# High and low parts of weights and activations side by side, two elements apart, at eight rotating offsets

## The chip, the cores and the metric

The kernel runs on one core of a Trainium2 chip. The metric is the device time of one execution in microseconds (us). Each execution computes one layer of an encoder trunk, from inputs in HBM to an output in HBM.

## The reference

All arithmetic is float32. Sequence length S is 256, model width D is 2048, MLP width 8192, and the memory has 256 tokens. The layer is a chain of matrix products with short work between them:

```python
h = rms_norm(x, norm_mix_g)
x = x + hybrid_mixer(h, ...)                       # one product with w_in (2048 x 18464), then w_out
h = rms_norm(x, norm_x_g); mem_n = rms_norm(mem, norm_mem_g)
x = x + cross_attention(h, mem_n, w_xq, w_xkv, w_xo)   # 4 heads
h = rms_norm(x, norm_ffn_g)
x = x + square(relu(h @ w_ff1)) @ w_ff2
return rms_norm(x, norm_final_g)
```

`hybrid_mixer` splits the product with w_in into a retention branch and a gated delta-rule branch, both worked in chunks along the sequence, gates them and adds them. Every weight is read once: 404 MB cross the DMA queue in one execution.

## The kernel before

A float32 product is made of three faster ones. Each operand is split into a high part, which is the value rounded to the format `float32r`, and a low part, which is the rest; high*high, high*low and low*high are summed in PSUM. ScalarE (ACT) makes the high part by a copy, VectorE (DVE) the low part by a subtraction.

**Weights.** `fetch` (L87) loads 1 MB of a weight matrix with one DMA into the tile `raw` (128 x 2048, three buffers) and splits it in two halves of 128 x 1024: L106 writes the high half `whi` on ACT, L107 the low half `wlo` on DVE. Both are tiles of their own with three buffers each. `whi` has room for 64 elements more, and in `blocks` it starts 56 elements (224 bytes) into its buffer (`AT_BLOCKS`); in `chunk` it starts at 0. All tile sizes of that pool are multiples of 256 bytes, so this fixes where each operand lies within a period of 256 bytes.

**Activations.** A `Quad` (L124) holds four k-tiles of the activations, feature-major. Its tile `both` is 128 x 4 x 512: for each k-tile first 256 high elements (one per token), then 256 low ones. Quads live in the pools `hq` (`quad_a`), `q2` (`quad_b`) and, for the memory's activations, `kv` (`memq`, L293). Two empty tiles, `PAD1` (8 elements) and `PAD2` (80), shift the last two pools.

**Two forms of a product.** TensorE (PE) loads a stationary operand of 128 x 128 (LDWEIGHTS, shown as PEld) and streams a moving operand of up to 512 columns past it; the load for the next matmul goes on while the present one streams.

- `blocks` (L171): the weights are stationary, the output is feature-major. Per k-tile and output block, L187 streams the whole 512 columns (high and low activations at once) past the high weights, and L188 streams the 256 high activations past the low weights. It makes the mixer's q, k, v and decay inputs, the memory's keys, w_out, w_xq, w_xo and the MLP's first product.
- `chunk` (L133): the activations are stationary, the output is token-major. Per k-tile and half of the tokens, L147, L148 and L149 stream 512 weight columns each: high*high, high*low, low*high. It makes the memory's values (4 calls, on `memq`), the mixer's values and gates (20 calls, on `h1`), and the MLP's second product (16 calls, on `hid`).

Each of these matmuls has its own LDWEIGHTS. The order of the instructions on each engine is set by the tile framework, which schedules with a simulated timeline and the priorities that the code gives; PE then works strictly in that order.

Of the kernel before, what the change touches and what calls it, by code (L numbers as in the profile page):

```python
# [11 lines left out]
F32R = mybir.dt.float32r  # L12
# [5 lines left out]
P = 128  # L18
D = 2048
S = 256  # L20
# [10 lines left out]
THETA = 10000.0  # L31


AT_BLOCKS = (56, 0)
PAD1, PAD2 = 8, 80
TWO_PI = 2.0 * math.pi
BIG = 1.0e30
# [14 lines left out]
def trunk(ctx: ExitStack, tc: tile.TileContext, x, mem, positions, norm_mix_g, w_in, conv_w, gdn_a_log, gdn_dt_bias,  # L52
# [8 lines left out]
    wp = ctx.enter_context(tc.tile_pool(name="wpipe", bufs=3))  # L61
    hqp = ctx.enter_context(tc.tile_pool(name="hq", bufs=1))
# [4 lines left out]
    def stream_ps():  # L67
        s0 = psp.tile([P, 512], F32, name="s0", tag="s0", bufs=2)
        s1 = psp.tile([P, 512], F32, name="s1", tag="s1", bufs=2)
        return s0, s1  # L70

    def bank():
        return psp.tile([P, 512], F32, name="b", tag="b", bufs=4)
# [4 lines left out]
    def step():  # L78
        if steps and next(steps[0], steps) is steps:
            steps.pop(0)  # L80
# [3 lines left out]
            step()  # L84


    def fetch(pieces, k, n, rush=False, hold=None, at=(0, 0)):  # L87


        raw = wp.tile([P, k * n], F32, name="raw", tag="raw", bufs=3)  # L90
        rv = raw.rearrange("p (k n) -> p k n", k=k)
        with tc.high_priority(offset=100000):
            for off, ap in pieces:
                src = ap.rearrange("(k p) n -> p k n", p=P)
                for ks in ((slice(0, k // 2), slice(k // 2, k)) if rush else (slice(0, k),)):
                    nc.sync.dma_start(rv[:, ks, off:off + ap.shape[1]], src[:, ks, :])
            got = []
            for i in range(2):
                if hold:
                    both = hold().both  # L100
                    hi, lo = (both[:, a:a + 2, :].rearrange("p a s -> p (a s)") for a in (0, 2))
                else:
                    hi, lo = (wp.tile([P, k * n // 2 + room], F32R, name=nm, tag=nm, bufs=3)[:, a:a + k * n // 2]
                              for nm, a, room in zip(("whi", "wlo"), at, (64, 0)))
                src = raw[:, i * k * n // 2:(i + 1) * k * n // 2]
                act.activation(hi, src, AF.Copy)  # L106
                vec.tensor_sub(lo, src, hi.bitcast(F32))  # L107
                got.append((hi.rearrange("p (k n) -> p k n", n=n), lo.rearrange("p (k n) -> p k n", n=n)))
        return got

    def split(dst, src, at=slice(None)):
        h, l = (a[:, at] for a in dst)
        act.activation(h, src, AF.Copy)
        vec.tensor_sub(l, src, h.bitcast(F32))
# [6 lines left out]
    class Quad(tuple):  # L121
        pass

    def new_quad(pl, bufs):  # L124
        both = pl.tile([P, 4, 2 * S], F32R, name="q", tag="q", bufs=bufs)
        quad = Quad((both[:, :, 0:S], both[:, :, S:2 * S]))
        quad.both = both
        return quad

    def quad_a():  # L130
        return new_quad(hqp, 5)

    def chunk(quads, pieces_of, evac, before=None, hold=None):  # L133


        ps = stream_ps()
        parts = [(t, 0, 512, ps[t]) for t in range(NT)]
        if hold:
            parts[1:] = [(1, 0, 256, ps[1][:, :256]), (1, 256, 512, bank()[:, :256])]
        held = {q: fetch(pieces_of(q), 4, 512, hold=hold) for q in ((2, 3) if hold else ())}  # L140

        def products(q, i, part, halves):
            t, c0, c1, o = part
            xh, xl = (a[:, i, t * P:(t + 1) * P] for a in quads[q])
            wh, wl = (a[:, i % 2, c0:c1] for a in halves[i // 2])
            first, last = q == 0 and i == 0, q == 3 and i == 3
            pe.matmul(o, xh, wh, start=first, stop=False)  # L147
            pe.matmul(o, xh, wl, start=False, stop=False)  # L148
            pe.matmul(o, xl, wh, start=False, stop=last)  # L149

        for q in range(4):
            if q not in held:
                if before:
                    before(q)
                halves = fetch(pieces_of(q), 4, 512, rush=before is not None and q == 0)
                for i in range(4):
                    for part in parts:
                        products(q, i, part, halves)
                    if i % 2:
                        step()  # L160
        for part in parts:
            for q, halves in held.items():
                for i in range(4):
                    products(q, i, part, halves)
            with tc.high_priority(offset=50000):
                evac(part[0], part[3], part[1], part[2])
# [4 lines left out]
    def blocks(quads, w, c0, nb, evac):  # L171

        k = 16 // nb
        ps = stream_ps()
        n = nb * P
        for g in range(KT // k):
            halves = fetch([(0, w[g * k * P:(g + 1) * k * P, c0:c0 + n])], k, n, at=AT_BLOCKS)
            for i in range(k):  # L180
                kk = g * k + i
                xh, xhl = quads[kk // 4][0][:, kk % 4, :], quads[kk // 4].both[:, kk % 4, :]
                wh, wl = halves[i // (k // 2)]
                for b in range(nb):
                    bs = slice(b * P, (b + 1) * P)
                    lh, ll = wh[:, i % (k // 2), bs], wl[:, i % (k // 2), bs]
                    pe.matmul(ps[b], lh, xhl, start=kk == 0, stop=False)  # L187
                    pe.matmul(ps[b][:, :S], ll, xh, start=False, stop=kk == KT - 1)  # L188
                if i % (k // 2) == k // 2 - 1:
                    step()  # L190
        for b in range(nb):
            with tc.high_priority(offset=50000):
                o = sm.tile([P, S], F32, name="bo", tag="bo", bufs=2)
                act.activation(o, ps[b][:, S:], AF.Copy)  # L194
                vec.tensor_add(o, o, ps[b][:, :S])  # L195
                evac(b, o)
# [73 lines left out]
    kv = kvs.enter_context(tc.tile_pool(name="kv", bufs=2))  # L270
# [19 lines left out]
    kt_d = dram.tile([P, KT, S], F32, name="kt_d", tag="kt_d", bufs=1)  # L290
    vv_d = dram.tile([P, NT, D], F32, name="vv_d", tag="vv_d", bufs=1)
    kv.tile([P, PAD1], F32, name="pad1", bufs=1)
    memq = [new_quad(kv, 4) for _ in range(4)]  # L293
    ssqm = cp.tile([P, NT, 4], F32, name="ssqm")

    def load_mem(c):
# [31 lines left out]
    for k2 in range(8):  # L328
# [10 lines left out]
        for f in range(2):  # L339
            k = 2 * k2 + f  # L340
# [160 lines left out]

    values(2)
    blocks(h1, w_in[0], C_GA, 1, decay_rows)
    values(3)
    for h in range(4):
# [6 lines left out]
    for b2 in range(8):  # L512
        ko = kv.tile([P, 2, S], F32, name="ko", tag="vo", bufs=2)

        def evac_k(b, ps):
            vec.tensor_mul(ko[:, b, :], ps, mrow)

        blocks(memq, w_xkv[0], b2 * 256, 2, evac_k)
        nc.sync.dma_start(kt_d[:, 2 * b2:2 * b2 + 2, :], ko)
        if b2 < 4:  # L520
            for h in (2 * b2, 2 * b2 + 1):
                decays(8 + h)
                ret_decays(h)
# [17 lines left out]
    def gdn_stream(grp):  # L541
# [3 lines left out]
        for pr in range(2):  # L545
# [5 lines left out]
            for part, c0, bofs in ((1, C_GQ, 0), (0, C_GK, 16), (2, C_GV, 32)):  # L551
                def evac(b, ps, part=part, bofs=bofs):
                    if part < 2:
                        conv_silu(bofs + h0 + b, ps, kq[:, b, part, :])
                    else:
                        vt = mx.tile([P, S], F32, name="vt", tag="vt", bufs=2)
                        conv_silu(bofs + h0 + b, ps, vt)
                        vts.append(vt)
                blocks(h1, w_in[0], c0 + h0 * GD, 2, evac)
# [260 lines left out]
    for j in range(5):  # L820
# [3 lines left out]
        if j:  # L824
            if j < 4:
                quad = mx.tile([P, 4, S], F32, name="mg", tag="mg", bufs=3)
                kept.append(quad)
            else:
                finish_steps()
                quad = quad_a()  # L830
# [21 lines left out]
    def quad_b():  # L852
        return new_quad(q2p, 4)
# [49 lines left out]
    for h in range(XH):  # L903
# [31 lines left out]
        quad = quad_a()  # L935
        for d2 in range(2):
            ops = bank()
            ov = ops.rearrange("p (d s) -> p d s", d=2)
            for d in range(2):
                c0 = (2 * d2 + d) * P  # L940
# [24 lines left out]
    for fb in range(4):  # L965
        hid = []
        for b2 in range(8):
            hs = fp.tile([P, 2, S], F32, name="hs", tag="hs", bufs=2)
            if b2 % 2 == 0:
                hid.append(quad_a())  # L970

            def evac_h(b, ps):
                vec.scalar_tensor_tensor(hs[:, b, :], ps, 0.0, ps, op0=ALU.max, op1=ALU.mult)  # L973
                qh, ql = (a[:, b2 % 2 * 2 + b, :] for a in hid[-1])
                act.activation(qh, hs[:, b, :], AF.Copy)  # L975
                vec.tensor_sub(ql, hs[:, b, :], qh.bitcast(F32))  # L976

            blocks(h3, w_ff1[0], fb * D + b2 * 256, 2, evac_h)
        for n in range(4):
# [13 lines left out]
            def evac_last(t, ps, c0, c1):  # L993
# [20 lines left out]
                for c in (0, 3, 1, 2):  # L1014
# [13 lines left out]
                  hold=quad_b if last else None)  # L1028
# [27 lines left out]
```

## Time and profile before

| | |
|---|---|
| runs | 2108.81 us median of 2 (2108.48 to 2109.13) |
| profiled execution | 2106.88 us, span of its instructions 2105.2 us |
| PE busy | 2083.3 us (99%), 11172 matmuls |
| DVE busy | 1407.7 us (67%) |
| ACT busy | 1091.6 us (52%) |
| DMA | 193 GB/s in the mean, queue q1 59.5% of 16 engines |
| granted TensorE clock | 0.999 |

In a row of the groups stand the line, engine and operation, then output and inputs by tile name, their shapes, the count, the busy time with the mean of one in ns, and the idle time of the engine before them with what ended it. A matmul's duration in the profile holds its latency through the array, so the rate of a stream of matmuls is read from the distance between their starts in the timeline, not from the duration.

### The profile page before, as it was taken

Reading aid. Unit: us, or ns where it says so; the run is one execution under the profiler, and the core shown is the slowest. Engines: PE = TensorE matmul, PEld = TensorE weight load, DVE = VectorE, ACT = ScalarE, POOL = GpSimd, SP = SyncE. Lnnn points to the kernel's source line nnn. Section 1 sums busy time; section 2 is a strip of 40 time slices with the busy share of each in tenths; the row PEclk is TensorE's granted clock in tenths of the full one; section 3 lists DMA queues with packets and bytes.
Section 4 is the critical chain, followed back from the end, with each engine's and each line's share of the span. In section 5 each row is a group of like instructions: output and inputs, shape, how many; then the busy total and the mean of one; then the engine's idle time right before and its main releaser. Section 6 shows DMA issues by size and latency. Waiting matters only on the chain.

```text
span 2105.2 us, 28781 instructions
## 1 busy us (share of the span) xinstructions
PE 2083.3 (99%) x11172; PEld 1796.9 (85%) x11172; DVE 1407.7 (67%) x2225; ACT 1091.6 (52%) x1700; POOL 28.7 (1%) x39
## 2 busy tenths in 40 slices
PE   8999999999999999999999999999999999999998
PEld 6878888888888888888888899888888888888887
DVE  6756779678758884878557666766556555645655
ACT  7565564565446454655355555554434434434444
POOL 0000000000000000000000000000000000000000
PEclk9999999999999999999999999999999999999999
DMA  8778655555545555555458654566566556556653
GB/s 298 243 242 258 201 181 193 176 171 182 184 156 193 192 175 166 182 183 190 153 174 256 202 186 155 180 197 186 199 190 191 197 187 197 188 192 198 185 198 140
DMA packets 316010, 405.91 MB, mean 193 GB/s; under 512 B 16593, under 2 KB 224481, under 8 KB 315745
## 3 DMA queue, kind: packets, MB, share of 16 engines
q1 hardware_dynamic: 315872, 404.08, 59.5%
q8 instruction: 87, 1.43, 0.3%
q14 instruction: 51, 0.41, 0.1%
HBM read 390.40 MB, written 13.65 MB: 192 GB/s over the span
## 4 chain that ended last, share of the span: by engine, by line
PE 93%; DMA 3%; ACT 2%; DVE 1%; SPq 1%; issue 0%; ACTq 0%; POOLq 0%; POOL 0%; DVEq 0%
PE s L187 32%; PE s L188 17%; PE s L148 13%; PE s L149 13%; PE s L147 13%; PE b L675 2%; DMA dec_d<-dec_w 1%; ACT whi L106 1%; DVE wlo L107 1%; ACT dec_w L493 1%; PE b L581 1%; DMA xc<-x 1%; PE b L117 0%; DMA xt_d<-xt 0%; PE b L119 0%; PE b L118 0%
## 5 line engine op out<-in xcount | busy, mean ns | idle before, releaser
L107 DVE TENSOR_TENSOR wlo<-raw,whi 128x1024 fp32r<-128x1024 f32 x702 | 858.3, 1223 | 522.0 <-ACT whi L106 516.2
L106 ACT ACTIVATE whi<-raw 128x1024 fp32r<-128x1024 f32 x702 | 742.3, 1059 | 730.9 <-PE s L149 387.0
L187 PE MATMUL s<-q,whi 128*128 128x512 f32 x3088 | 1063.4, 390 | 0.7 <-ACT whi L106 0.4
L188 PE MATMUL s<-q,wlo 128*128 128x256 f32 x3088 | 845.3, 281 | 5.2 <-DVE wlo L107 5.1
L187 PEld LDWEIGHTS s<-q,whi 128*128 128x128 f32 x3088 | 570.8, 188 | 111.5 <-ACT whi L106 1.6
L188 PEld LDWEIGHTS s<-q,wlo 128*128 128x128 f32 x3088 | 579.0, 188 | 20.1 <-DVE wlo L107 8.8
L148 PE MATMUL s<-wlo,q 128*128 128x512 f32 x1264 | 495.6, 392 | 1.0 <-DVE wlo L107 1.0
L149 PE MATMUL s<-whi,q 128*128 128x512 f32 x1264 | 492.4, 390 | 0.0
L147 PE MATMUL s<-whi,q 128*128 128x512 f32 x1264 | 454.1, 391 | 0.0
L148 PEld LDWEIGHTS s<-wlo,q 128*128 128x128 f32 x1264 | 238.0, 188 | 50.1 <-DVE wlo L107 2.5
L147 PEld LDWEIGHTS s<-whi,q 128*128 128x128 f32 x1264 | 237.5, 188 | 49.2 <-ACT q L249 0.4
L149 PEld LDWEIGHTS s<-whi,q 128*128 128x128 f32 x1264 | 237.6, 188 | 48.0
L194 ACT ACTIVATE bo<-s 128x256 f32<-128x256 f32 x193 | 73.1, 379 | 118.8 <-PE s L188 105.9
L195 DVE TENSOR_TENSOR bo<-bo,s 128x256 f32<-128x256 f32 x193 | 80.4, 417 | 44.4 <-ACT bo L194 44.1
L534 DVE SCALAR_TENSOR_TENSOR acc<-bo,cw,acc 128x255 f32<-128x255 f32 (+2 forms) x144 | 66.8, 480 | 1.5
L636 DVE TENSOR_TENSOR pr<-lw,tw 32x31 f32<-32x31 f32 (+15 forms) x124 | 40.4, 325 | 8.4 <-DMA lw<-scr_l 6.5
L638 DVE TENSOR_TENSOR tw<-tw,pr 32x31 f32<-32x31 f32 (+15 forms) x124 | 40.5, 327 | 2.1
L782 ACT ACTIVATE gth<-s 128x512 f32<-128x512 f32 x32 | 18.9, 591 | 22.5 <-PE s L149 18.3
L984 DVE SCALAR_TENSOR_TENSOR res<-s,rstd3q,res 128x512 f32<-128x512 f32 (+1 forms) x32 | 22.3, 735 | 11.8 <-PE s L149 11.8
L973 DVE SCALAR_TENSOR_TENSOR hs<-bo 128x256 f32<-128x256 f32 x64 | 27.0, 422 | 1.1
L976 DVE TENSOR_TENSOR q<-hs,q 128x256 fp32r<-128x256 f32 x64 | 26.8, 419 | 0.8 <-ACT q L975 0.8
L531 ACT ACTIVATE acc<-bo,cw 128x256 f32<-128x256 f32 x48 | 24.1, 503 | 4.5 <-DVE bo L195 4.4
(292 smaller groups left out, 1084.3 us busy)
## 6 DMA issues: line engine op xcount, KB each, us to landing
raw<-w_in SPq DMA_DIRECT2D x144, 1024.0 KB, 5.1
raw<-w_ff SPq DMA_DIRECT2D x128, 1024.0 KB, 5.4
raw<-w_xkv SPq DMA_DIRECT2D x31, 1024.0 KB, 5.9
raw<-w_out SPq DMA_DIRECT2D x16, 1024.0 KB, 5.7
raw<-w_xq SPq DMA_DIRECT2D x16, 1024.0 KB, 6.5
raw<-w_xo SPq DMA_DIRECT2D x16, 1024.0 KB, 5.5
dec_d<-dec_w SPq DMA_DIRECT2D x16, 192.0 KB, 4.0
dec<-dec_d SPq DMA_DIRECT2D x8, 384.0 KB, 3.2
```

Source lines behind the costliest of these rows:

```text
L106: act.activation(hi, src, AF.Copy)
L107: vec.tensor_sub(lo, src, hi.bitcast(F32))
L147: pe.matmul(o, xh, wh, start=first, stop=False)
L148: pe.matmul(o, xh, wl, start=False, stop=False)
L149: pe.matmul(o, xl, wh, start=False, stop=last)
L187: pe.matmul(ps[b], lh, xhl, start=kk == 0, stop=False)
L188: pe.matmul(ps[b][:, :S], ll, xh, start=False, stop=kk == KT - 1)
L194: act.activation(o, ps[b][:, S:], AF.Copy)
L195: vec.tensor_add(o, o, ps[b][:, :S])
L534: vec.scalar_tensor_tensor(acc[:, d:], ps[:, :S - d], cw[:, j, blk:blk + 1], acc[:, d:], op0=ALU.mult, op1=ALU.add)
L638: vec.tensor_sub(tw[:, j + 1:32, 0:j + 1], tw[:, j + 1:32, 0:j + 1], pv)
L675: pe.matmul(pv[:, i, :], lhs(i), rhs[:, i, :], start=True, stop=True)
```

## The change

The high and the low part of a tile now lie in one tile, element by element (high, low, high, low, ...), for the weights of `blocks`, for the MLP's hidden activations and for the memory's activations. Every operand that reads one part then has a step of two elements (8 bytes). The weights of `chunk`, and the activations `h1`, `h2`, `h3`, the attention's and the merged ones keep one part behind the other.

- As **stationary** operands with that step: the weights in all calls of `blocks` (L187, L188, now L202, L203), and the activations in 20 of 40 calls of `chunk` (L147 to L149, now L161 to L163): 16 of the MLP, 4 of the memory.
- As **moving** operands with that step: `memq` in the 8 calls of `blocks` that make the memory's keys.
- The tiles `whi` and `wlo` become one tile `w` (128 x 2112, three buffers). Its parts start at an offset that goes through eight values, 0 to 56 elements in steps of 8, from one call of `blocks` or `chunk` to the next; `AT_BLOCKS` goes. The two pads stay as they are.

```diff
-AT_BLOCKS = (56, 0)
+AT_WEIGHTS = (0, 8, 16, 24, 32, 40, 48, 56)
...
+                    w = wp.tile([P, 2 * half + 64], F32R, name="w", tag="w", bufs=3)[:, at:at + 2 * half]
+                    w = w.rearrange("p (n e) -> p e n" if mixed else "p (e n) -> p e n", e=2)
+                    hi, lo = w[:, 0], w[:, 1]
                 act.activation(hi, src, AF.Copy)
                 vec.tensor_sub(lo, src, hi.bitcast(F32))
...
+    def next_at():
+        used.append(0)
+        return AT_WEIGHTS[len(used) % len(AT_WEIGHTS)]
...
+    def sides(both, mixed):
+        return both.rearrange("p f (s e) -> p f e s" if mixed else "p f (e s) -> p f e s", e=2)
...
-            halves = fetch([(0, w[g * k * P:(g + 1) * k * P, c0:c0 + n])], k, n, at=AT_BLOCKS)
+            halves = fetch([(0, w[g * k * P:(g + 1) * k * P, c0:c0 + n])], k, n, at=at, mixed=True)
...
-                xh, xhl = quads[kk // 4][0][:, kk % 4, :], quads[kk // 4].both[:, kk % 4, :]
+                xh, xhl = quads[kk // 4][0][:, kk % 4, :], quads[kk // 4].pair[:, kk % 4]
...
-    memq = [new_quad(kv, 4) for _ in range(4)]
+    memq = [new_quad(kv, 4, mixed=True) for _ in range(4)]
...
-                hid.append(quad_a())
+                hid.append(quad_a(mixed=True))
```

The number and the sizes of the matmuls, splits and DMAs stay the same. The schedule moves a little. On PE, in a call of `blocks` for the memory's keys (`s0`, `s1` are the two output blocks, `q` the activations), the order before was:

```order
827 L187 MATMUL s0_1901<-q_98,whi_1905 128x512
828 L188 MATMUL s0_1901<-q_98,wlo_1906 128x256
829 L187 MATMUL s1_1902<-q_98,whi_1905 128x512
830 L188 MATMUL s1_1902<-q_98,wlo_1906 128x256
831 L187 MATMUL s0_1901<-q_98,whi_1905 128x512
```

and it is now:

```order
827 L202 MATMUL s0_1843<-q_98,w_1847 128x512
828 L202 MATMUL s1_1844<-q_98,w_1847 128x512
829 L203 MATMUL s0_1843<-q_98,w_1847 128x256
830 L203 MATMUL s1_1844<-q_98,w_1847 128x256
831 L202 MATMUL s0_1843<-q_98,w_1847 128x512
```

At the first k-tile of a new half of weights the two products with the high part now stand ahead of the two with the low part; after that the pairs alternate as before. Two products with the high part followed each other at 141 places of `blocks` before, at 298 now.

More of the change, by code (lines that the diff above doesn't have):

```diff
@@ L84, in finish_steps, with fetch @@
             step()
-    def fetch(pieces, k, n, rush=False, hold=None, at=(0, 0)):
+    def fetch(pieces, k, n, rush=False, hold=None, at=0, mixed=False):
         raw = wp.tile([P, k * n], F32, name="raw", tag="raw", bufs=3)
@@ L97, in fetch @@
             got = []
+            half = k * n // 2
             for i in range(2):
+                src = raw[:, i * half:(i + 1) * half]
                 if hold:
@@ L102, in fetch @@
                 else:
-                    hi, lo = (wp.tile([P, k * n // 2 + room], F32R, name=nm, tag=nm, bufs=3)[:, a:a + k * n // 2]
-                              for nm, a, room in zip(("whi", "wlo"), at, (64, 0)))
-                src = raw[:, i * k * n // 2:(i + 1) * k * n // 2]
+                    w = wp.tile([P, 2 * half + 64], F32R, name="w", tag="w", bufs=3)[:, at:at + 2 * half]
+                    w = w.rearrange("p (n e) -> p e n" if mixed else "p (e n) -> p e n", e=2)
+                    hi, lo = w[:, 0], w[:, 1]
                 act.activation(hi, src, AF.Copy)
@@ L109, in fetch @@
         return got
+    used = []
+    def next_at():
+        used.append(0)
+        return AT_WEIGHTS[len(used) % len(AT_WEIGHTS)]
     def split(dst, src, at=slice(None)):
@@ L122, in trunk, with new_quad, quad_a @@
         pass
-    def new_quad(pl, bufs):
+    def sides(both, mixed):
+        return both.rearrange("p f (s e) -> p f e s" if mixed else "p f (e s) -> p f e s", e=2)
+    def new_quad(pl, bufs, mixed=False):
         both = pl.tile([P, 4, 2 * S], F32R, name="q", tag="q", bufs=bufs)
-        quad = Quad((both[:, :, 0:S], both[:, :, S:2 * S]))
-        quad.both = both
-        return quad
-    def quad_a():
-        return new_quad(hqp, 5)
+        pair = sides(both, mixed)
+        quad = Quad((pair[:, :, 0], pair[:, :, 1]))
+        quad.both, quad.pair = both, pair
+        return quad
+    def quad_a(mixed=False):
+        return new_quad(hqp, 5, mixed)
     def chunk(quads, pieces_of, evac, before=None, hold=None):
@@ L139, in chunk @@
             parts[1:] = [(1, 0, 256, ps[1][:, :256]), (1, 256, 512, bank()[:, :256])]
+        at = next_at()
         held = {q: fetch(pieces_of(q), 4, 512, hold=hold) for q in ((2, 3) if hold else ())}
@@ L154, in chunk @@
                     before(q)
-                halves = fetch(pieces_of(q), 4, 512, rush=before is not None and q == 0)
+                halves = fetch(pieces_of(q), 4, 512, rush=before is not None and q == 0, at=at)
                 for i in range(4):
@@ L177, in blocks @@
         n = nb * P
+        at = next_at()
         for g in range(KT // k):
-            halves = fetch([(0, w[g * k * P:(g + 1) * k * P, c0:c0 + n])], k, n, at=AT_BLOCKS)
+            halves = fetch([(0, w[g * k * P:(g + 1) * k * P, c0:c0 + n])], k, n, at=at, mixed=True)
             for i in range(k):
                 kk = g * k + i
-                xh, xhl = quads[kk // 4][0][:, kk % 4, :], quads[kk // 4].both[:, kk % 4, :]
+                xh, xhl = quads[kk // 4][0][:, kk % 4, :], quads[kk // 4].pair[:, kk % 4]
                 wh, wl = halves[i // (k // 2)]
```

## The prediction

> **What bounds the kernel now.** I read the page first, for shares and groups, then the list of waits of PE, then PE's timeline for the rate of its matmuls, and last the busy times by window for the engines that feed it.
>
> ```profile
> span 2105.2 us, 28781 instructions
> PE 2083.3 (99%) x11172; PEld 1796.9 (85%) x11172; DVE 1407.7 (67%) x2225; ACT 1091.6 (52%) x1700; POOL 28.7 (1%) x39
> L107 DVE TENSOR_TENSOR wlo<-raw,whi 128x1024 fp32r<-128x1024 f32 x702 | 858.3, 1223 | 522.0 <-ACT whi L106 516.2
> L106 ACT ACTIVATE whi<-raw 128x1024 fp32r<-128x1024 f32 x702 | 742.3, 1059 | 730.9 <-PE s L149 387.0
> L187 PE MATMUL s<-q,whi 128*128 128x512 f32 x3088 | 1063.4, 390 | 0.7 <-ACT whi L106 0.4
> L188 PE MATMUL s<-q,wlo 128*128 128x256 f32 x3088 | 845.3, 281 | 5.2 <-DVE wlo L107 5.1
> L148 PE MATMUL s<-wlo,q 128*128 128x512 f32 x1264 | 495.6, 392 | 1.0 <-DVE wlo L107 1.0
> ```
>
> PE has work in 99% of the span. The idle time just before its large groups is 0.7, 5.2 and 1.0 us. The splits wait for PE instead: ACT stood idle 387.0 us until an L149 had released a buffer. So what PE needs per matmul sets the time, and everything else matters only if it makes PE wait. The rate of a matmul is the distance between starts. In the MLP's first product (`blocks`):
>
> ```profile
> 1428.08 0.39 PE L187 MATMUL s<-q,whi 128*128 128x512 f32 x1
> 1428.31 0.28 PE L188 MATMUL s<-q,wlo 128*128 128x256 f32 x1
> 1428.42 0.39 PE L187 MATMUL s<-q,whi 128*128 128x512 f32 x1
> ...
> 1433.24 0.39 PE L187 MATMUL s<-q,whi 128*128 128x512 f32 x1
> ```
>
> and at the end of a `chunk`, where a call of `blocks` follows, at two places:
>
> ```profile
> 505.29 0.39 PE L149 MATMUL s<-whi,q 128*128 128x512 f32 x1
> 505.52 0.39 PE L147 MATMUL s<-whi,q 128*128 128x512 f32 x1
> 505.75 0.39 PE L148 MATMUL s<-wlo,q 128*128 128x512 f32 x1
> 505.97 0.40 PE L149 MATMUL s<-whi,q 128*128 128x512 f32 x1
> 506.21 0.39 PE L187 MATMUL s<-q,whi 128*128 128x512 f32 x1
> ...
> 1744.31 0.39 PE L147 MATMUL s<-whi,q 128*128 128x512 f32 x1
> ...
> 1745.44 0.40 PE L149 MATMUL s<-whi,q 128*128 128x512 f32 x1
> 1745.68 0.39 PE L187 MATMUL s<-q,whi 128*128 128x512 f32 x1
> ```
>
> From 1428.08 to 1433.24 stand 15 pairs of L187 and L188: 5.16 / 15 = 0.344 us a pair. In `chunk`, 505.29 to 505.97 is three matmuls, 0.227 us each, and 1744.31 to 1745.44 is five, 0.226 each. If a 512-column stream takes 0.227 in `blocks` as well, the 256-column one takes 0.117. The second 256 columns then cost 0.110, so of each matmul about 0.117 - 0.110 = 0.007 us does not grow with its length.
>
> The last matmul of each chunk is the one to look at. Its own weights lie at offset 0 of their buffer; while it streams, PE loads the first weights of `blocks`, which lie 224 bytes further in the period. It takes 0.24 us at both places, against 0.227 and 0.226 just before. The timeline's last digit is 0.01 us, so I count this as 0.008 more: about the mean of the two, cut a little for the rounding. In the streams of 0.227 both operands lie at the same place of the period. So the trace shows that a load which lies elsewhere than the stream can slow the stream by a few per cent. It shows no operand of PE with a step of two.
>
> **The change, part by part.** The instructions, their sizes and the DMAs stay. What changes is how PE reads, how ACT and DVE write, and where things lie.
>
> *Stationary operands with the step: blocks.* All 3088 L187 and 3088 L188 now stream past weights that were loaded with a step of 8 bytes over 1024 bytes instead of 512, at eight offsets in turn. Bound below: the load and the stream no longer touch, and the 0.007 us that does not grow with the length goes: 3088 x 2 x 0.007 = 43 us gained. Bound above: the load passes twice as many bytes, and each stream pays the 0.008 twice: 3088 x 2 x 0.016 = 99 us lost. The nearest row is the 0.24: a load out of place. With a step the load moves through the period differently from the stream, so I take its price, 0.008, for every 512-column stream: 3088 x 0.008 = 24.7 us. The 256-column stream already runs beside a load that lies 224 bytes away and takes 0.117, no more than the slope gives; for it I take 0.002, near its lower bound: 6.2 us.
>
> *Stationary operands with the step: chunk.* 20 of 40 calls, each 16 k-tiles x 2 halves x 3 = 96 matmuls of 512 columns, 1920 in all, on `hid` and `memq`. The same price: 1920 x 0.008 = 15.4 us; by the same bounds 13 us gained (0.007) to 31 us lost (0.016).
>
> *Rotating offsets where nothing has a step.* The other 20 calls of chunk keep contiguous operands on both sides, but only one offset in eight is the old one. 1920 x 7/8 x 0.008 = 13.4 us, the one term with a row for its very mechanism. Lower bound: 0, if 224 bytes is a bad place and most others are not.
>
> *Moving operand with the step.* Only the memory's keys: 8 calls x 16 k-tiles x 2 = 256 streams of 512 and 256 of 256 columns, 256 x 0.344 = 88 us now. Bounds: nothing, and once more the whole 88 us if a stream with a step runs at half the rate. No row is near; since the same 128 x 256 numbers are read from the same bytes in both passes, I stay near the lower end with 5 us.
>
> *The splits.* ACT writes 1024 elements in 1.06 us (L106), DVE subtracts in 1.22 (L107), 702 times each, of which 386 now write (and DVE also reads) with the step. I cost this at nothing. The cover is that DVE works 67% of the span and waits on ACT, which waits on PE. Where it is thinnest:
>
> ```profile
> 235.00:330.00 95.00, 95.00 (x531) 82.83 (x530) 78.24 (x158) 58.17 (x107) 2.01 (x2) 1.00 0.59 190
> 1402.00:1490.00 88.00, 88.00 (x511) 77.74 (x510) 54.49 (x79) 45.74 (x71) 0.64 (x1) 1.00 0.61 191
> ```
>
> These are the mixer's first streams and one first product of the MLP; the columns after the length are busy time of PE, PEld, DVE, ACT and POOL. DVE is busy 78.24 of 95 us in the one, 54.49 of 88 in the other. What it costs without that cover stands under the rivals.
>
> *One buffer for both parts.* A buffer of `w` comes free when both parts are used up, where `whi` could go a matmul earlier. In the trace PE's waits for the splits are
>
> ```profile
> PE s L188 <- DVE wlo L107: 5.1, 7, 1.6
> PE s L148 <- DVE wlo L107: 1.0, 2, 0.7
> ```
>
> 5.1 and 1.0 us in all, with three buffers ahead, so a release that comes one L188 (0.117 us) later stays hidden; and the two products with the high part that now stand first at a new half give DVE another 0.227 us before its part is wanted. If it did show, it would do so at each of those 7 places first, by 0.117 us each: under 1 us.
>
> The sum: 24.7 + 6.2 + 15.4 + 13.4 + 5 = 64.7 us. The profiled execution took 2106.9 us on the device, 1.7 over its span; the median of the runs is 1.9 above it. 2106.9 + 64.7 + 1.9 = 2173.5; I say **2172 us**, 3.0% slower. A measurement of this kernel tells about 2% from no change, 42 us.
>
> **Rivals.**
>
> *Faster: the step takes the load out of the stream's way.* If the 0.007 us of every matmul is the load and the stream meeting at the same place, a load that passes the period at another rate meets it less. All 8096 matmuls with a stepped stationary operand would win up to 0.007: 56.7 us, against which the offsets of the 20 plain calls and the keys still cost some. 2108.8 - 56.7 = 2052 us. It decides from 0.0052 us a matmul on (42 / 8096). For it: the 256-column stream beside a load 224 bytes away is not slowed, so out of place is not bad everywhere. Against: the only other row out of place is slower.
>
> *No change: load and stream do not disturb each other.* Then the 0.007 is the price of changing from one matmul to the next, the 0.24 has to do with the change of form from `chunk` to `blocks`, and the step and the offsets are free. 2109 us, up to 2150 with some of the smaller terms. For it: ACT, DVE and DMA work beside PE at changing addresses all the time and the rate is still 0.227 at 505 us and 0.226 at 1744 us. Against: the 0.24 at both places. The Trainium skill states this as a rule: in "SBUF — State Buffer" (section on the two sides of SBUF) PE has two independent read ports, one for the moving operand and one for the weights, and the same page puts the loss at fewer than two hits on a 16-byte line, which a step of two float32 elements just avoids. By it the whole sum would be zero; the trace does not settle it, since the 0.24 speaks against and nothing in it has a step.
>
> *Slower by DVE.* If the subtraction with steps took twice 1.22 us, 386 of them would add 471 us to DVE's 1407.7. In the mixer's window 6 calls of blocks with 4 halves each add 24 x 1.22 = 29 us where 16.8 are free: 12 us lost, four times, 50 us. In the MLP's window 8 calls add 39 us to 54.49 of 88: 5.5 us, four times, 22 us. With some 30 us in the 24 calls of w_out, w_xq and w_xo, whose output also costs DVE several operations, about 100 us: 2210. Against: nothing in the trace shows steps slowing DVE.
>
> *The order.* That the scheduler's shift itself costs PE time is not a case of its own: 298 pairs of high products instead of 141 stream the same columns.
>
> **How the numbers follow.** The forecast, reads that disturb each other more than now, gets 0.41, the slowing by DVE or by a half-rate moving operand 0.07. No change gets 0.29, faster 0.23. So: faster by over 2% 0.23, within 2% 0.29, slower by over 2% 0.48. The range reaches to the faster case at 2052 below. Above it takes the stepped reads at their upper bounds and the plain chunks at their price, 99 + 31 + 13.4 = 143 us over 2109, which makes 2252 and holds the DVE case too; the upper bound of the keys on top of that is left out. I give 2050 to 2255. The forecast's own range is 2152 to 2240.
>
> **What would show it.** In the timeline after, pairs of blocks at 0.352 to 0.356 us instead of 0.344, and chunks of the mixer's gates at 0.235 in most calls and 0.227 in about one of eight, show the forecast's steps. Pairs that differ from call to call by the offset show that the place matters also with a step. Pairs at 0.330 or less mean the faster rival; 0.344 everywhere, no change. The keys' stage shows the moving operand by itself. L107 should keep 1.22 us in the mean; if it grows and PE's wait for DVE rises from 5 us to tens, DVE was the place. The forecast is wrong if the pairs of blocks get no longer, since half its sum rests on them.

## The result, and the profile after

| kernel | time (us, median) | span of the profiled execution |
|---|---|---|
| before | 2108.81 | 2105.2 |
| changed | 2223.33 (2223.32 to 2223.34) | 2221.6 |

The changed kernel takes 1.0549 times as long (95% interval 1.0528 to 1.0570): 5.5% slower. The page after, with the rows that answer to those of before:

```profile
span 2221.6 us, 28590 instructions
PE 2205.0 (99%) x11172; PEld 1871.2 (84%) x11172; DVE 1410.3 (63%) x2225; ACT 1130.5 (51%) x1700; POOL 28.6 (1%) x39
L109 DVE TENSOR_TENSOR w<-raw,w 128x1024 fp32r<-128x1024 f32 x702 | 859.2, 1224 | 635.2 <-ACT w L108 632.8
L108 ACT ACTIVATE w<-raw 128x1024 fp32r<-128x1024 f32 x702 | 776.2, 1106 | 811.2 <-PE s L163 402.2
L202 PE MATMUL s<-q,w 128*128 128x512 f32 x3088 | 1143.2, 418 | 0.5 <-DVE q L960 0.5
L203 PE MATMUL s<-q,w 128*128 128x256 f32 x3088 | 854.7, 293 | 0.0
L162 PE MATMUL s<-w,q 128*128 128x512 f32 x1264 | 500.9, 396 | 0.6 <-DVE w L109 0.6
```

PE is still busy 99% of a longer span, and it hardly waits before its large groups: 0.5, 0.0 and 0.6 us. DVE's subtraction is unchanged (1223 to 1224 ns). ACT's copy grew from 1059 to 1106 ns in the mean, and ACT waits longer for PE than before. So the 116 us that the span grew by are in the matmuls themselves. The timeline of PE shows two different losses. In the memory's keys, where the moving operand has the step:

```profile
202.09 0.63 PE L202 MATMUL s<-q,w 128*128 128x512 f32 x1
202.55 0.41 PE L203 MATMUL s<-q,w 128*128 128x256 f32 x1
202.78 0.63 PE L202 MATMUL s<-q,w 128*128 128x512 f32 x1
...
204.83 0.63 PE L202 MATMUL s<-q,w 128*128 128x512 f32 x1
```

Four pairs take 2.74 us, 0.685 each, where a pair of `blocks` took 0.344: 0.455 for the 512 columns, 0.23 for the 256, twice as long for both. In the MLP's first product, where only the stationary operand has the step, two calls at different offsets:

```profile
1545.99 0.40 PE L202 MATMUL s<-q,w 128*128 128x512 f32 x1
...
1548.15 0.64 PE L202 MATMUL s<-q,w 128*128 128x512 f32 x2
...
1577.09 0.39 PE L202 MATMUL s<-q,w 128*128 128x512 f32 x1
...
1578.84 0.39 PE L202 MATMUL s<-q,w 128*128 128x512 f32 x1
```

Six pairs in 2.16 us make 0.360; five in 1.75 make 0.350. The loss is 2 to 5% and depends on the offset. And the gates of the mixer, where no operand has a step and only the offset changes from call to call:

```profile
451.98 0.39 PE L162 MATMUL s<-w,q 128*128 128x512 f32 x1
...
453.57 0.39 PE L163 MATMUL s<-w,q 128*128 128x512 f32 x1
...
680.33 0.39 PE L161 MATMUL s<-w,q 128*128 128x512 f32 x1
...
681.73 0.40 PE L161 MATMUL s<-w,q 128*128 128x512 f32 x1
```

Seven matmuls in 1.59 us, 0.227 each, in a call whose weights lie in place; six in 1.40, 0.233 each, in a call where they lie elsewhere in the 256 bytes.

### The profile page after: what moved, and what is told of

Its sections match the earlier page's. It is cut to its first block, busy times and chain, and to the rows that moved or that the text cites. A ratio compares the mean times of both kernels' runs of the same rounds, so it can differ in the third digit from the quotient of the medians.

```text
span 2221.6 us, 28590 instructions
## 1 busy us (share of the span) xinstructions
PE 2205.0 (99%) x11172; PEld 1871.2 (84%) x11172; DVE 1410.3 (63%) x2225; ACT 1130.5 (51%) x1700; POOL 28.6 (1%) x39
## 4 chain that ended last, share of the span: by engine, by line
PE 98%; DMA 1%; SPq 0%; DVE 0%; issue 0%; ACT 0%; ACTq 0%; POOLq 0%; POOL 0%; DVEq 0%
PE s L202 35%; PE s L203 18%; PE s L162 13%; PE s L163 13%; PE s L161 13%; PE b L690 1%; PE b L596 1%; DMA xc<-x 1%; PE b L125 0%; PE b L127 0%; PE b L126 0%; SPq L298 0%; PE b L682 0%; PE b L598 0%; DMA invf<-inv_freq 0%; PE b L594 0%
## 5 line engine op out<-in xcount | busy, mean ns | idle before, releaser
L109 DVE TENSOR_TENSOR w<-raw,w 128x1024 fp32r<-128x1024 f32 x702 | 859.2, 1224 | 635.2 <-ACT w L108 632.8
L108 ACT ACTIVATE w<-raw 128x1024 fp32r<-128x1024 f32 x702 | 776.2, 1106 | 811.2 <-PE s L163 402.2
L202 PE MATMUL s<-q,w 128*128 128x512 f32 x3088 | 1143.2, 418 | 0.5 <-DVE q L960 0.5
L203 PE MATMUL s<-q,w 128*128 128x256 f32 x3088 | 854.7, 293 | 0.0
L202 PEld LDWEIGHTS s<-q,w 128*128 128x128 f32 x3088 | 590.6, 198 | 134.0 <-issue 46.6
L203 PEld LDWEIGHTS s<-q,w 128*128 128x128 f32 x3088 | 610.2, 198 | 36.2 <-issue 12.4
L162 PE MATMUL s<-w,q 128*128 128x512 f32 x1264 | 500.9, 396 | 0.6 <-DVE w L109 0.6
L163 PE MATMUL s<-w,q 128*128 128x512 f32 x1264 | 497.9, 395 | 0.0
L161 PE MATMUL s<-w,q 128*128 128x512 f32 x1264 | 457.9, 395 | 0.2 <-ACT w L108 0.2
L162 PEld LDWEIGHTS s<-w,q 128*128 128x128 f32 x1264 | 242.5, 192 | 49.8 <-DVE w L109 1.0
L161 PEld LDWEIGHTS s<-w,q 128*128 128x128 f32 x1264 | 241.6, 192 | 50.7 <-ACT w L108 0.6
L163 PEld LDWEIGHTS s<-w,q 128*128 128x128 f32 x1264 | 242.5, 192 | 49.1
L990 ACT ACTIVATE q<-hs 128x256 fp32r<-128x256 f32 x64 | 27.5, 429 | 0.0
```

## The experiments

Two theories came out of this. A: a moving float32r operand with a step of two elements streams at half the rate, and that is most of the loss. D: the rest is the place of the load against the stream within 256 bytes, with a step or without.

**1. The memory plain.** The changed kernel without the step in the memory's activations.

```diff
-    memq = [new_quad(kv, 4, mixed=True) for _ in range(4)]
+    memq = [new_quad(kv, 4) for _ in range(4)]
```

> The changed kernel with the memory's activations laid out as before (256 high, then 256 low elements), all else as changed. Theory A: a moving operand with a step of two float32r elements streams at half the rate, so the 256 pairs of the memory's keys (0.453 + 0.229 us after, 0.227 + 0.118 before) carry 86 us of the loss. Then 2223 - 86 = 2137 us, pairs of the keys back at about 0.35. Rival B: the keys are slow because stationary and moving operand both have a step and collide. Then this run is 2137 too, and e2 tells them apart. Rival C: the keys' stage is slow for its supply (DVE, DMA), not for its reads: 2220.

2146.4 us; 1.0188 (1.0171 to 1.0205) times the kernel before, which took 2106.3 in these rounds. 40 us of the loss stay, where the expectation left 28; the step of the memory's activations carries the rest of the 115, some 75 us. About half of the miss is waiting: PE idles 5.5 us before L203 for L109 in this run, and 0.0 us in the changed kernel. Rival C, the supply of that stage, falls.

**2. The memory's step alone.** The kernel before, with its weights as they were and only `memq` interleaved (`sides`, `pair` and `mixed=True` for `memq`, as in the change).

> The kernel before with only the memory's activations interleaved; the weights keep whi and wlo, contiguous, at their old offsets. A (half rate by the moving step alone): 2109 + 86 + 384 matmuls of the memory's values with a stepped stationary operand x 0.005 = 2197 us. B (it takes both steps): 2111 us.

2184.4 us, 1.0370 (1.0355 to 1.0386): 78 us lost to one part of the change, with contiguous weights. In its keys' stage:

```profile
202.02 0.64 PE L191 MATMUL s<-q,whi 128*128 128x512 f32 x1
202.47 0.41 PE L192 MATMUL s<-q,wlo 128*128 128x256 f32 x1
202.70 0.64 PE L191 MATMUL s<-q,whi 128*128 128x512 f32 x1
...
204.06 0.64 PE L191 MATMUL s<-q,whi 128*128 128x512 f32 x1
```

Three pairs in 2.04 us, 0.68 each. So the moving step suffices by itself, and B, that it takes steps on both sides, falls. I had expected 88 us, not 78. 256 pairs x (0.68 - 0.344) are 86 us, and PE is indeed busy 84.1 us longer than before (2167.4 against 2083.3). But it is idle 6.2 us less: some of the loss is paid back in the same stage, where PE had been short of split weights. Before, it waited 5.1 us for an L107 ahead of an L188; in this run no such wait is left in the list:

```profile
L191 PE MATMUL s<-q,whi 128*128 128x512 f32 x3088 | 1134.8, 411 | 0.3 <-DVE q L949 0.3
L192 PE MATMUL s<-q,wlo 128*128 128x256 f32 x3088 | 878.1, 292 | 0.0
```

**3. The offsets alone.** The changed kernel with no step anywhere: `mixed=True` removed in `blocks`, for `memq` and for `hid`. One tile for both parts and the eight offsets stay.

> The changed kernel with no step anywhere: one tile w, high part then low part, at eight rotating offsets, all activations as before. Theory D (the rest of the loss is the place within 256 bytes: in the trace after, contiguous 512-column streams take 0.227 in place and 0.229 to 0.234 out of place): about 5900 of 6880 streams out of place x 0.0048 = 28 us: 2137 us. Rival E (the rest is the step of the stationary operand, wherever it lies): 1900 plain chunk matmuls x 7/8 x 0.005 = 8 us at the most: 2109 to 2117 us.

2136.8 us, 1.0143 (1.0128 to 1.0158), 30.6 us over the kernel before: D's number, and far from E's. Some three quarters of the 40 us come with no step at all. In the MLP's second product:

```profile
1539.62 0.40 PE L162 MATMUL s<-w,q 128*128 128x512 f32 x1
...
1541.49 0.63 PE L161 MATMUL s<-w,q 128*128 128x512 f32 x2
```

Eight matmuls in 1.87 us: 0.234, with contiguous operands on both sides.

But run 1 has the same offsets and takes 9.6 us more than this run (2146.4 against 2136.8), and their intervals do not touch. What differs is the step of the load and of the splits that write it, and PE is busy 10.8 us longer (2122.8 against 2112.0). So D's "with a step or without" is too strong: the step has a price of its own.

**4. The step at one fixed offset.** As 1, with `AT_WEIGHTS = (0,)`.

> As e1_memory_plain, with one fixed offset of 0 for all weights: plain chunks are back in place, blocks and the MLP's second product keep stepped stationary operands, 0 or 4 bytes from the stream's place. Theory D: the plain chunks get 0.227 again (9 us less than e1), the stepped ones stay out of place in any case: the stepped load starts in place but leaves it. In the trace after 4 bytes away still takes 0.233: 4540 x 0.005 = 23 us: 2131 us. Rival E gives about the same here, 2131. Rival F (a step is free once load and stream start at the same place): 2110 us.

2143.1 us, 1.0173 (1.0158 to 1.0188): 37 us over the kernel before, more than the 23 expected. Rival F, that a step is free once load and stream start at the same place, falls. The MLP shows what the step and the offsets cost apart, since PE does nothing else there. The starts of its rows give the length of the first product (256 pairs of `blocks`) and the second product (384 matmuls of `chunk`) of the MLP's second quarter, in us:

| | first product | second product |
|---|---|---|
| before, from 1570.31 to 1658.61 to 1745.68 | 88.30 | 87.07 |
| run 3, offsets without a step, from 1589.17 to 1678.84 to 1767.81 | 89.67 | 88.97 |
| run 1, the same offsets with the step, from 1597.16 to 1687.57 to 1777.06 | 90.41 | 89.49 |
| run 4, the step at offset 0, from 1589.25 to 1679.91 to 1770.37 | 90.66 | 90.46 |

In the first product the offsets cost 1.37 us and the step 0.74 more, 0.003 us a pair; over the 3088 pairs of `blocks` that is 8.9 of the 9.6 us between runs 3 and 1. In the second product the step's own price does not show clearly: 0.5 us more here, 0.2 less in the next quarter (89.09 against 89.26). But with the step, offset 0 takes longer than the rotating offsets (0.236 a matmul), although it is where contiguous operands are fastest. Why stays open.

**5. The rates by themselves.** A kernel of its own, run once: cases of 64 matmuls, back to back, on operands of `x`, with nothing else running.

> A measurement by itself, with none of the reference's work: cases of 64 matmuls each, back to back, with one stationary and one moving operand, and nothing else running. The time of a matmul is (busy time of the case minus the last one's duration) / 63. float32r, 512 columns, both operands contiguous: in place (inplace) 0.227; 32 to 192 bytes apart (bytesq 32, bytesr 64, bytess 96, bytest 128, bytesu 192) 0.230 to 0.234, and 0.227 again at 256 and 512 (bytesv, bytesw) if the period is 256 bytes (theory D). Stationary operand with a step of 2, 4, 8 elements (loadtwo, loadfour, loadeight): 0.233 by D for all three; a rival, that each further line touched costs more, gives 0.233, 0.246, 0.272. Moving operand with a step of 2, 3, 4, 8 (movetwo to moveeight): theory A gives 0.453 for 2; for the larger ones 0.453 if a neighbour is wasted, more if bytes passed count. pairs (two neighbours of every four elements) and lines (four of every eight) tell the unit fetched: 0.227 for pairs if it is 8 bytes; 0.453 for pairs and 0.227 for lines if it is 16; 0.453 for both if bytes passed count. float32 at 256 columns (wholeplain, wholetwo, wholefour; half the bytes per time): 0.215 with steps 1 and 2 if the unit is 8 bytes. bfloat16 at 512 columns (shortplain, shorttwo, shortfour, shorteight: 2, 4, 8, 16 bytes apart): 0.215 to 0.227 up to 4 bytes, twice that at 8 if the unit alone decides.

The timeline merges each case into a row: start, busy time, then the case's name as the output tile. The time of a matmul is also the distance from a start to the next row's start, divided by the count (float32 takes two passes, so x128).

```profile
30.70 14.68 PE L50 MATMUL inplace<-mr,sr 128*128 128x512 f32 x64
45.21 15.09 PE L50 MATMUL bytesq<-mr,sr 128*128 128x512 f32 x64
60.14 15.10 PE L50 MATMUL bytesr<-mr,sr 128*128 128x512 f32 x64
...
104.93 14.82 PE L50 MATMUL bytesu<-mr,sr 128*128 128x512 f32 x64
119.59 14.68 PE L50 MATMUL bytesv<-mr,sr 128*128 128x512 f32 x64
134.10 14.67 PE L50 MATMUL bytesw<-mr,sr 128*128 128x512 f32 x64
148.62 15.10 PE L50 MATMUL loadtwo<-mr,sr 128*128 128x512 f32 x64
163.55 15.21 PE L50 MATMUL loadfour<-mr,sr 128*128 128x512 f32 x64
178.59 15.80 PE L50 MATMUL loadeight<-mr,sr 128*128 128x512 f32 x64
194.23 7.83 PE L50 MATMUL halfplain<-mr,sr 128*128 128x256 f32 x64
201.90 15.63 PE L50 MATMUL halfloadeight<-mr,sr 128*128 128x256 f32 x64
217.37 29.04 PE L50 MATMUL movetwo<-mr,sr 128*128 128x512 f32 x64
246.22 28.98 PE L50 MATMUL movethree<-mr,sr 128*128 128x512 f32 x64
275.01 29.71 PE L50 MATMUL movefour<-mr,sr 128*128 128x512 f32 x64
304.53 27.78 PE L50 MATMUL moveeight<-mr,sr 128*128 128x512 f32 x64
332.12 29.06 PE L50 MATMUL pairs<-mr,sr 128*128 128x512 f32 x64
361.00 15.11 PE L50 MATMUL lines<-mr,sr 128*128 128x512 f32 x64
375.95 27.79 PE L50 MATMUL wholeplain<-raw 128*128 128x256 f32 x128
403.58 29.17 PE L50 MATMUL wholetwo<-raw 128*128 128x256 f32 x128
432.59 57.91 PE L50 MATMUL wholefour<-raw 128*128 128x256 f32 x128
490.32 14.00 PE L50 MATMUL shortplain<-mb,sbf 128*128 128x512 bf16 x62
504.15 14.62 PE L50 MATMUL shorttwo<-mb,sbf 128*128 128x512 bf16 x63
518.61 10.55 PE L50 MATMUL shortfour<-mb,sbf 128*128 128x512 bf16 x23
```

- *Place.* In place 14.51 / 64 = 0.227. 32 bytes away 0.233, 192 bytes away 0.229, and at 256 and 512 bytes 0.227 again: the period is 256 bytes, as D has it.
- *Step of the load.* Two elements 0.233, four 0.235, eight 0.244 beside 512 columns. The rival that each further line costs more asked for 0.246 and 0.272. Beside 256 columns a step of eight takes 0.242 against 0.120, about the same as beside 512: there the load sets the rate.
- *Step of the stream.* Two elements 0.451, three 0.450, four 0.461, eight 0.431, so more distance costs no more. `pairs`, two neighbours of every four elements, takes 0.451 as well; `lines`, four neighbours of every eight, 0.234. The unit that counts is therefore 16 bytes: a float32r stream that skips a part of each unit takes twice as long, and one that skips whole units hardly more than a contiguous one.
- *Width.* float32 at 256 columns takes 0.216 a pass, 0.227 with a step of two, 0.451 with four. bfloat16 takes 0.216 contiguous and 0.226 with a step of two (14.46 us from start to start over its 64 matmuls, two of which the records lack in the one case and one in the other), and 0.451 with four (10.55 us less a last duration of 0.63, over 22). Contiguous, both bear about half the bytes of float32r per time, and both can skip every second element nearly for nothing.

The rows that touch 128 units of 16 bytes take 0.226 to 0.227 (inplace, wholetwo, shorttwo) or 0.234 (lines); four rows that touch 256 (movetwo, pairs, wholefour, shortfour) take 0.451. That is some 1.76 ns a unit, and a contiguous float32r stream is already at it. The price does not carry further: a float32r step of three touches 384 units, steps of four and eight 512, and all three stay between 0.431 and 0.461. For float32r alone another reading fits all rows within 5%: one column per 0.88 ns (0.451 / 512) as soon as a unit is not used whole. Which of the two it is stays open; both give the changed kernel's keys the same time. bfloat16 with a step of eight ran mostly while the granted clock stood at half (5 tenths in the page's last four of 40 slices) and isn't used.

**6. The same tile in the order in which it lies.** The changed kernel, with the keys streaming `memq` as 512 contiguous columns:

```diff
+                    if quads[0].mixed:
+                        pe.matmul(ps[b], lh, quads[kk // 4].both[:, kk % 4, :], start=kk == 0, stop=False)
+                        pe.matmul(ps[b], ll, quads[kk // 4].both[:, kk % 4, :], start=False, stop=kk == KT - 1)
+                        continue
...
+                low, high = (ps[b][:, 1:2 * S:2], ps[b][:, 0:2 * S:2]) if quads[0].mixed else (ps[b][:, S:], ps[b][:, :S])
```

> The changed kernel, but the memory's keys stream the same interleaved tile in the order in which it lies: 512 contiguous columns (high, low, high, low) past the high weights, and the same 512 past the low weights, which adds the product of the two low parts. The output's columns then alternate too, and the two instructions that read them out of PSUM step by two. Theory A (the rate is set by how many 16-byte lines a stream passes; step two passes twice as many): both streams take 0.233, the pair 0.466 instead of 0.682: 256 x 0.216 = 55 us less than the changed kernel, 2168 us on a chip where that takes 2223, less some us if PE waits for its supply in that stage again. A rival (interleaved tiles are slow to read in any order, by how they were written or where they lie): 0.453 for both, 0.9 the pair: 2280.

2176.7 us, 1.0330 (1.0313 to 1.0347), 46 us less than the changed kernel took in its own rounds.

```profile
179.70 0.39 PE L203 MATMUL s<-q,w 128*128 128x512 f32 x1
179.94 0.40 PE L204 MATMUL s<-q,w 128*128 128x512 f32 x1
...
182.49 0.40 PE L203 MATMUL s<-q,w 128*128 128x512 f32 x1
...
PE s L204 <- DVE w L109: 7.3, 7, 2.7
```

Six pairs in 2.79 us: 0.465, as A has it. The interleaved tile is not slow to read; skipping half of it is. PE waits 7.3 us for DVE again, which is most of the gap between 55 and 46: when the keys stream faster, the stage is short of split weights again.

No run points to a version that beats the kernel before: the contiguous form in place has the lowest time of the float32r cases of run 5.

## Why the prediction was right in direction, and where its sum was wrong

- **Direction and range.** Forecast 2172 us and slower, in 2050 to 2255; measured 2223. What bounds the kernel was read rightly: PE's rate per matmul, with the splits hidden. DVE's 1224 ns and its longer idle time show it; ACT's 47 ns more cost next to nothing, since PE waited only 0.2 us for L108.
- **What was luck.** The upper end of the range was built from loads at twice the price, which no run shows, and it left out the upper bound of the keys, which is most of what happened. Without the keys the loss is 40 us, 1.9% (run 1), just under the 2% that the chances were given for. A half-rate moving operand shared a chance of 0.07 with DVE.
- **The step that failed: the moving operand.** It was given bounds of 0 and 88 us and a value of 5, on the ground that both passes read the same bytes. The upper bound was right: 0.68 instead of 0.344 for 256 pairs, 86 us, of which run 2 shows 78 in the time. Nothing in the trace of before was near this row, and the reason given for the low end was an argument and no row. Run 5 answers it: 512 columns with a step of two take 0.451, as long as two whole streams, so two passes over the same bytes cost two reads of them.
- **The load out of place.** This was the right mechanism, shown by run 3 without any step (30.6 us). The 0.008 does not follow from the rows shown with it: 0.24 stands 0.013 above 0.227. It still came out for the 512-column streams of `blocks`: 90.41 instead of 88.30 us for 256 pairs is 0.008 a pair, of which the place makes 0.005 and the step 0.003. In `chunk` it was too large: 89.49 instead of 87.07 us for 384 matmuls is 0.006. The sign that it named, pairs of 0.352 to 0.356, came as 0.353 in that stage of run 1, and as 0.350 and 0.360 in two calls of the changed kernel. The forecast's four terms for the load come to 59.7 us; run 1, which has them all but for the step of the memory's four calls of `chunk`, lost 40.
- **The 256-column stream.** Forecast 0.002 more; it keeps 0.117: in the call at 1577 us a pair takes 0.350, of which a 512-column stream out of place takes 0.233.
- **Two errors of opposite sign.** 20 us too much on the load and some 70 too little on the keys leave the forecast 51 us short. (Its sum stands at 2173.5 and was given as 2172 without a reason.)
- **Rivals.** *Faster* falls: run 5's stepped load, alone with its stream, takes 0.233. *No change* falls with run 3. The rule cited beside it, from the Trainium skill ("SBUF — State Buffer", the specifications and the note on cachelines: two hits on a 16-byte line keep the full bandwidth), does not hold here for PE's moving operand in float32r: a step of two elements has two hits a line and takes 0.451 instead of 0.227. In float32 the same step takes 0.227 instead of 0.216. Of independent ports the runs show only that the place of the load moves a stream from 0.227 to 0.234. *DVE* falls at 1224 ns. *The order* made no difference that shows: L203 before its L109 waits 5.7 us in run 3, 5.1 before.

## What to carry to other kernels

Price an access pattern for each reader of a tile, stationary and moving apart: the same step cost 0.006 us a matmul on one side and 0.224 on the other (run 5). A contiguous float32r stream had no room for skipped elements, where float32 and bfloat16 had it: a step of two took 0.451 instead of 0.227 in the one, and 0.227 and 0.226 instead of 0.216 in the others. Where the trace has no row for a cost and its bounds lie far apart, a small measurement of that one pattern, or the middle of the bounds, serves better than an argument for one end.

## What had not been expected of the hardware

- The unit that counts in a stream's reads is 16 bytes, whether float32r, float32 or bfloat16 is read: 0.226 to 0.227 for 128 units and 0.451 for 256 in seven cases of run 5. More units cost a float32r stream no more: 0.450, 0.461 and 0.431 for 384, 512 and 512.
- A load disturbs a stream by where it starts within 256 bytes: 0.227 in place, up to 0.234 elsewhere, 0.229 at 192 bytes.
- A step of two in the load costs a little beyond its place: 0.003 us a pair in `blocks` between runs 3 and 1, and at offset 0 the MLP's second product takes 0.236 a matmul, where contiguous operands take 0.227.
- A load with a step of eight elements takes about 0.24 us and then sets the rate of 256-column matmuls (0.242 instead of 0.120). With a step of two the 256-column streams of the whole kernel keep their 0.117.
